# Scores of q's low parts as two 64-row matmuls, one on each half of the TensorE array

## The chip, the cores and the metric

One NeuronCore of a Trainium2 chip runs the whole program. The metric is the device time of one execution in microseconds. TensorE (PE in the profile) does matmuls and loads their weights (PEld), VectorE (DVE), ScalarE (ACT) and GpSimd (POOL) the rest; SyncE (SP) issues the DMAs.

## What is computed

Three blocks over 1024 tokens of width 1024. Two attentions over all keys are what the change is about:

```python
# layer 0, differential attention: 8 heads, two parts c of 64 per head
sc = jnp.einsum('bqhcd,bkhcd->bhcqk', qb, k, preferred_element_type=f32) * scale
p = jax.nn.softmax(sc, axis=-1)
p = p[:, :, 0] - lam * p[:, :, 1]
...
# layer 1, MLA: 8 heads, 128 features of their own and 64 roped ones, k_pe shared by the heads
sc = (jnp.einsum('bqhd,bkhd->bhqk', qn, k_nope, preferred_element_type=f32)
      + jnp.einsum('bqhr,bkr->bhqk', qp, k_pe, preferred_element_type=f32)) * scale
p = jax.nn.softmax(sc, axis=-1)
```

A third block follows (gating, causal and dilated attentions, an FFN), which the change leaves alone.

## The kernel before

Every fp32 operand x of a matmul is held as two fp32r tiles, a first part hi = round(x) and a second part lo = x - hi, so that a product is the sum of hi hi, hi lo and lo hi; `mm3` (L192) writes these three matmuls per 128 rows of contraction.

Where the contraction has 64 rows, the parts are stacked instead. In layer 0 `qk_rope` (L620) makes for each part s of a head the keys `kk[s]`, 128 rows by 1024 keys, with hi in rows 0 to 63 and lo in rows 64 to 127, and the queries `q[s](hl, j)`, 128 rows by 128 queries, in which the same part hl stands in both halves of the rows. It moves them there from the roped tiles `ab` by small DMAs on SP's queue (`move`, L675). `score` (L678) then needs two matmuls per 512 keys: q hi (L681) and q lo (L682) against the stack, all four products. A score row of `da_attention` (L847 on; 128 queries by 1024 keys, one PSUM tile `s` of two banks) is four matmuls; each of 8 heads has 8 query tiles times 2 parts, 128 rows in all. In layer 1 `mla_attention` (L1076) does the same for the 64 rope features with `kpe`, the stacked k_pe of all heads, and `qp`: per 512 keys three matmuls for the 128 features of the head (L1093 to L1095), then q's rope hi (L1096) and lo (L1097) against `kpe`. There a score row is ten matmuls, and there are 64.

A row then goes through `exp_row`: maximum on VectorE (L737, L738), exponential on ScalarE (L741), reciprocal (L742). `pt_fill` transposes it on TensorE (L757), ScalarE and VectorE split the transposes, and `pv` multiplies by v (L192). There are two PSUM tiles `s`.

Head h's attention is emitted in steps, with the projections of head h + 1 and the modulation of later layers as fill between them (`merge`, `alternate`); `ahead` lets the attention's instructions be scheduled before work emitted a little earlier. A list scheduler of the framework then sets the order on each engine from these priorities, so an edit of one matmul shifts others too. Within an engine and on SP's queue everything runs in that order.

The matmuls of few rows in the program before are in set-up alone: `columns` (L234) transposes vectors of 86, 56, 62, 88 and 44 rows, and `modulation_first` has sixteen one-row matmuls twice (L359).

Of the kernel before, what the change touches and what calls it, by code (L numbers as in the profile page):

```python
# [36 lines left out]
    dict(h4=20, kk=5, qq=5, ab=2, pt=12, e=6, v=3, z=3, wr=2, wh=3, wl=3, tb=3, t2=4, tf=3),  # L37
    dict(h4=18, kk=4, qq=6, ab=3, pt=12, e=6, v=3, z=3, wr=4, wh=3, wl=2, tb=3, t2=2, tf=4),
# [6 lines left out]
def alternate(a, b):  # L45
    """steps of a and of b together"""
    for _ in a:
        next(b, None)
        yield
    yield from b  # L50
# [7 lines left out]
def ahead(tc, gen, offset):  # L58
    """steps of gen, scheduled before work that was emitted up to offset instructions earlier"""
    if not offset:  # L60
        yield from gen
        return
    while True:
        with tc.high_priority(offset):
            x = next(gen, drain)
        if x is drain:
            return
        yield x


def some(g, n):
    """n steps of g"""
    for _ in range(n):
        if next(g, drain) is drain:
            return
        yield


def merge(main, fill, lead=0):
    """emit one step of fill after each step of main"""  # L80
    for _ in range(lead):
        next(fill, None)
    for _ in main:
        next(fill, None)
    drain(fill)


def pace(main, total, early, fill, n):
    """steps of early at once, then n steps of fill spread over main, whose steps give their weight"""
    w = done = 0  # L90
    for x in main:
        w += x or 1
        if next(early, 0) == 0:
            while done < n * w / total:
                next(fill, None)
                done += 1
    drain(early)
    drain(fill)


class Net:
# [18 lines left out]
    def load(self, tag, shape, dt=F32):  # L120
        """a tile to be loaded, but not long before its phase"""
# [10 lines left out]
    def t(self, tag, shape, dt=F32):  # L132
        """a tile of 4 KB a partition, seen in the shape"""
# [14 lines left out]
    def c(self, shape, name, dt=F32):  # L148
        """a constant, or columns that stay"""
        r = dt == F32R  # L150
        n = 1 if r else shape[1]
        if name not in self.where:
            self.where[name] = self.used[r]
            self.used[r] += n
        o = self.where[name]
        return self.cr[:, o] if r else self.cf[:, o:o + n]

    def small(self, cols, tag):
        """columns for a short time: the next of a few in turn"""
# [11 lines left out]
    def wblock(self, src, k, m, lo_eng=None):  # L171
        """src: DRAM [k*128, m]; returns [(hi, lo)] per contraction chunk, each [128, m]"""
        return self.wload([src], k, m, lo_eng)

    def wload(self, srcs, k, m, lo_eng=None):
        """blocks of columns side by side"""
# [10 lines left out]
    def mm3(self, out, ws, rs, start=True, stop=True):  # L187
        """out += sum_k ws[k]^T rs[k]; ws, rs: (hi, lo)"""
# [26 lines left out]
    def columns(self, tile_name, width, names):  # L215
        """vectors as columns [128, j]"""
# [23 lines left out]
    def mask_tile(self, name, op, pattern, mult):  # L240
        """0 where the condition holds, else -BIG"""
# [39 lines left out]
    def sigmoid(self, sg, z, src):  # L281
        """sg <- sigmoid(z); src: where |z| is read from (z or its PSUM source)"""
# [15 lines left out]
    def modulation(self, cs, w, bcol, names, acc_tag="t2", w_tag="wr", shared=()):  # L298
        """columns [128, 8] of each 1024 outputs of cs @ w + b; chunks in shared: on ScalarE and GpSimd"""
# [27 lines left out]
    def sum_cols(self, acc, out):  # L327
        """out [128, 8] <- sums over the partitions of acc"""
# [7 lines left out]
    def modulation_first(self, cs, w, bcol, g, nme, acc_tag, w_tag):  # L336
        """as modulation, half of the products on TensorE"""
# [24 lines left out]
    def scale_col(self, g, scale, name):  # L362
        """g * (1 + scale)"""
# [14 lines left out]
    def stat_sum(self, acc):  # L378
        """sum over partitions, on every partition (PSUM)"""
# [10 lines left out]
    def rsqrt_mean(self, out, sums, dim):  # L390
        """(sums / dim + eps)^-1/2"""
# [5 lines left out]
    def stat_end(self, acc, dim):  # L397
        """acc -> (sum over partitions / dim + eps)^-1/2 on every partition, in place"""
        return self.rsqrt_mean(acc, self.stat_sum(acc), dim)

    def new_xt(self, tags):
        """x^T of a token half: 8 chunks [128, 512] in len(tags) tiles"""
# [37 lines left out]
    def operand(self, x, tag="h4", eng=None):  # L440
        """x [128, 512], split"""
# [5 lines left out]
    def rows(self, w, c0, m=128):  # L447
        """loads columns c0.. of w as the rows of a block, by halves of the contraction"""
# [8 lines left out]
    def weights(self, load, early):  # L457
        """operands of two blocks of rows by the number of the product, the first two products' first"""
# [20 lines left out]
    def strassen(self, load, ops, box, tag, early=False):  # L479
        """two blocks of rows times h, [128, 1024] each; early: the products of the first token half, alone,  # L480
        in steps"""
# [31 lines left out]
    def next_h(self, proj, xbox, acc, acol, shift):  # L513
        """ends the projection; h of the next part (fp32, in the place of x), and the operands of its first
        token half"""
# [16 lines left out]
    def turn_ops(self, ops, b11, b12, b21, b22):  # L532
        """operands of a chunk of each half of the contraction, but the first two products'; in place"""
# [11 lines left out]
    def start_pairs(self, pair, n, chunk, ops):  # L545
        """the first pairs of blocks: what needs the first token half, the other operands, the rest"""
# [13 lines left out]
    def load_x(self):  # L560
        """tokens of x"""
# [8 lines left out]
    def turn_x(self, toks):  # L570
        """x^T of the token halves, and their normalisation as rows on every partition"""
# [31 lines left out]
    def rope_half(self, psa, psb, half, outs):  # L603
        """outs: Ah, Al, Bh, Bl views"""
# [15 lines left out]
    def qk_rope(self, w, qcol, kcol, hts, perm=1):  # L620
        """q, k of two 64-wide heads, roped, split and stacked for the scores: kk[s], q[s](hl, q tile)"""
# [18 lines left out]
        for half in range(2):  # L640
# [11 lines left out]
            for s in range(2):  # L652
# [4 lines left out]
                for d in range(2):  # L657
                    for i in range(2):
                        r = slice(64 * d + 32 * i, 64 * d + 32 * i + 32)
                        ks, qs = slice(64 + 32 * s, 96 + 32 * s), slice(32 * s, 32 * s + 32)  # L660
                        if perm == 1:
                            self.move(kk[s][r, half * 512:half * 512 + 512], ab[i][ks, d])
                            self.move(qt[s][half][r], ab[i][qs])
                        elif half:
# [13 lines left out]
    def score(self, ps, q, j, kk, ks, stop=True):  # L678
        """ps = q tile j . keys ks, all four products of the parts"""
# [4 lines left out]
    def v_tiles(self, w, cols, k, rs, perm=1, pair=False):  # L684
        """v [key, 128] of the columns, split: [128, hl, 8, 128], or pair: [128, 8, 2, hl, 64]"""
# [31 lines left out]
    def silu_blocks(self, w, cols, hts, box):  # L717
        """silu(h @ w[:, c:c + 128])^T for c in cols, fp32 [128, 1024]"""
# [14 lines left out]
    def exp_row(self, ps, scale):  # L733
        """softmax numerator and reciprocal of its sum"""
# [13 lines left out]
    def pt_fill(self, pts, p, slot, ktiles):  # L748
        """transposes of p[:, k tiles] into column slot; pts = [hi 0-1, lo 0-1, hi 2-3, ..]"""
# [14 lines left out]
    def pv(self, v, pts):  # L764
        """O^T [128, 512]"""
# [5 lines left out]
    def out_proj(self, w, ots, gcol, xs_in, xs_out, half, tags, stats, accs, box):  # L771
        """x' = x + gate * (o @ w) for a token half, in T layout; stats: column factors (or None) of accs"""
# [18 lines left out]
    def keep_o(self, o):  # L791
        """o^T chunk, split"""
# [11 lines left out]
    def load_o(self, od, half, cs, ots, fac=None):  # L804
        """chunks cs of o^T of a token half from DRAM, split"""
# [17 lines left out]
    def last_head(self, att, w0, w1, early, loads, proj, hold=0):  # L823
        """the attention of the last head; fill in its first half (of weight w0): early and the loads of
        the first half's o^T, in its second: the output projection of the first half (but hold steps,
        which come with the loads of the second half's o^T)"""
# [20 lines left out]
    def da_attention(self, h, kk, q, box, od, ots=None):  # L847
# [6 lines left out]
        for half in range(2):  # L854
            pts = self.pt_new()
            for slot in range(4):
                es = []
                for s in range(2):
                    ps = self.pS()
                    for kh in range(2):  # L860
                        ks = slice(kh * 512, kh * 512 + 512)
                        self.score(ps[:, ks], q[s], half * 4 + slot, kk[s], ks)
# [37 lines left out]
    def layer0(self):  # L900
# [25 lines left out]
        def qk(h, box):  # L926
            box.append((yield from self.qk_rope(w, h * 128, 1024 + h * 128, hts)))
# [41 lines left out]
    def lora_norm(self, w, c0, n, dim, gcol, hts, tags, box):  # L969
        """rmsnorm of h @ w[:, c0:c0+128n], as (hi, lo) tiles [half][block]"""  # L970
# [28 lines left out]
    def mla_kpe(self, w, c0, hts, kd):  # L999
        """roped k_pe^T stacked [hi (x1, x2); lo (x1, x2)]"""  # L1000
# [18 lines left out]
    def mla_qpe(self, wq, qa, qpe):  # L1019
        """roped q_pe of all heads -> DRAM [head, hl, 64, 1024]"""  # L1020
# [24 lines left out]
    def split_psum(self, ps, dst):  # L1045
        """dst [128, 2, 512] <- exact parts of ps"""
# [29 lines left out]
    def mla_attention(self, h, qn, qp, kn, vbox, kpe, zd, od, ots=None):  # L1076
        nc = self.nc
        scale = 192.0 ** -0.5
        for half in range(2):
# [4 lines left out]
            for slot in range(4):  # L1084
# [4 lines left out]
                for kh in range(2):  # L1089
# [7 lines left out]
                    nc.tensor.matmul(o, qp[1][:, qs], kpe[:, ks], start=False, stop=True)  # L1097
# [9 lines left out]
    def layer1(self, hts):  # L1107
# [34 lines left out]
        nc.sync.dma_start(kpe.bitcast(F32), kd)  # L1142
        od = self.scratch([8, 128, S], "od1")
# [11 lines left out]
        for h in range(7):  # L1155
            cur, box, vbox = box, [], []
            fill = alternate(chain(self.mla_v(h, a["w_kv_b"], ckv, vbox), head(h + 1, box)), some(mods, 4))
            merge(ahead(self.tc, self.mla_attention(h, *cur, vbox, kpe, zd, od), HP_M), fill)
        drain(mods)
        m2 = self.mod  # L1160
        for nme in ("gate_m", "gate_f"):
# [16 lines left out]
            self.mla_attention(7, *cur, vbox, kpe, zd, od, ots), 4, 4, self.mla_v(7, a["w_kv_b"], ckv, vbox),  # L1178
# [22 lines left out]
    def gelu(self, ps, dst):  # L1201
        """tanh-form gelu of ps into dst (SBUF)"""
# [11 lines left out]
    def mixer_a(self, w, hts, od):  # L1214
        nc, a = self.nc, self.a
        # causal w_sp, transposed and split
# [12 lines left out]
        for b in range(2):  # L1229
# [6 lines left out]
            # v: [s, g, n, c], group norm  # L1236
# [41 lines left out]
    def mixer_b_qk(self, w, p, hts, box):  # L1278
        """q, k of the heads of pair p"""
# [26 lines left out]
    def fold(self, ps, y, e):  # L1306
        """y rows of head e <- sum of the two row halves of ps"""
# [55 lines left out]
    def mixer_c_attention(self, g, d, kk, q, vbox, lse, od):  # L1363
# [4 lines left out]
        for e in range(2):  # L1368
# [61 lines left out]
            # lse = max * scale + ln(sum), 1 / sum; to token order  # L1430
# [17 lines left out]
    def alphas_c(self, lse, fac):  # L1448
        """softmax of lse over the 3 groups, over the softmax sum; [6, 1024] in token order"""
# [80 lines left out]
    def ffn(self, hs, ops):  # L1530
        """the convolved gate and val in pairs of blocks, and their product, kept in DRAM; then the product
        with w_down"""
# [47 lines left out]
    def down(self, half, k1, k2, act, ys):  # L1580
        """x + gate * (act @ w_down) for a token half, in T layout; ys: the chunks before k1"""
# [39 lines left out]
    def finish(self, xt, half):  # L1621
        """rmsnorm of x in token layout, with g_final"""
# [68 lines left out]
```

## Time and profile before

| | us |
|---|---|
| median of 3 runs | 3095.03 |
| lowest and highest run | 3091.07, 3096.70 |
| profiled execution, span from its first to its last instruction | 3102.5 |
| TensorE busy, matmul / weight load | 2673.2 (86%) / 2154.1 (69%) |
| VectorE busy | 2110.7 (68%) |
| ScalarE / GpSimd busy | 1434.4 (46%) / 1292.2 (42%) |
| layer 0's attention | about 90 to 786 |
| layer 1's attention | about 1100 to 1612 |

No other time of the profiled execution is given than its span; it is longer than the highest of the three runs by 5.8 us. Busy times are unions of an engine's instructions; the ends of matmuls are modelled, so that two that follow each other overlap in the list, and the distance from start to start is what one takes in a stream. The granted clock is the share of full speed (2.4 GHz) that TensorE was given; the lower of its two levels is 1.2 GHz.

### The profile page before, as it was taken

What the parts mean: (1) busy time and instruction counts of PE and PEld (TensorE: products, weight loads), DVE (VectorE), ACT (ScalarE), POOL (GpSimd) and SP (SyncE); (2) the same over time, 40 slices, a digit from 0 to 9 for tenths busy, and PEclk for the clock granted to TensorE, in tenths of its full rate; (3) what the DMA queues carried; (4) which work ended last, traced back from release to release, by engine and by line L of the source; (5) the groups of instructions that cost most, each with busy time, mean ns of one, the idle gap of its engine ahead of it and who ended that gap; (6) DMA issues with size and microseconds to landing.
All of it is one profiled execution on the core that took longest, in us unless ns stands there. A gap on an engine that the chain in (4) does not pass through costs nothing. (4 is left out here: it accounts for less than half of the span.)

```text
span 3102.5 us, 34630 instructions
## 1 busy us (share of the span) xinstructions
PE 2673.2 (86%) x12023; PEld 2154.1 (69%) x12023; DVE 2110.7 (68%) x2888; ACT 1434.4 (46%) x2609; POOL 1292.2 (42%) x775
## 2 busy tenths in 40 slices
PE   7899999999989957778789689888887999998897
PEld 4677777777767746567667567777675777776776
DVE  7787778766653365555566756377876888889865
ACT  5455554556444423334345444366743444444332
POOL 2323333223353522112124333244545877787761
PEclk8999999999999978889899899999998999998998
DMA  7433333224441352321334235533361222224664
GB/s 268 132 93 96 105 94 90 72 67 118 122 122 53 117 178 78 100 83 53 103 106 131 68 81 82 107 82 100 97 195 46 77 82 75 82 89 149 210 213 153
DMA packets 316225, 338.90 MB, mean 109 GB/s; under 512 B 37060, under 2 KB 239892, under 8 KB 316052
## 3 DMA queue, kind: packets, MB, share of 16 engines
q1 hardware_dynamic: 316052, 336.69, 37.0%
q8 instruction: 96, 1.57, 0.2%
q14 instruction: 77, 0.63, 0.1%
HBM read 231.17 MB, written 60.89 MB: 94 GB/s over the span
## 5 line engine op out<-in xcount | busy, mean ns | idle before, releaser
L192 PE MATMUL m<-h,wh 128*128 128x512 f32 x4744 | 1399.6, 404 | 59.3 <-ACT wh L183 18.6
L192 PEld LDWEIGHTS m<-h,wh 128*128 128x128 f32 x4744 | 912.1, 195 | 269.3 <-ACT wh L183 21.0
L192 PE MATMUL m<-h,wl 128*128 128x512 f32 x1472 | 590.3, 403 | 10.1 <-POOL wl L169 10.0
L169 POOL TENSOR_TENSOR wl<-wr,wh 128x1024 fp32r<-128x1024 f32 (+1 forms) x146 | 329.4, 2263 | 577.6 <-PE m L192 184.4
L761 ACT CAST pt<-m 128x256 fp32r<-128x256 f32 (+1 forms) x632 | 221.2, 369 | 367.8 <-DVE pt L169 192.1
L192 PEld LDWEIGHTS m<-h,wl 128*128 128x128 f32 x1472 | 286.5, 195 | 75.3 <-POOL wl L169 12.5
L169 DVE TENSOR_TENSOR pt<-m,pt 128x256 fp32r<-128x256 f32 (+2 forms) x652 | 256.8, 416 | 103.2 <-ACT pt L761 81.7
L741 ACT ACTIVATE e<-s,cf 128x1024 f32<-128x1024 f32 x192 | 214.8, 1120 | 163.6 <-DVE cf L738 140.2
L737 DVE TENSOR_REDUCE cf<-s 128x1 f32<-128x1024 f32 x192 | 232.6, 1218 | 70.6 <-PE s L682 38.6
L757 PE MATMUL m<-cr,e 128*128 128x128 f32 x1240 | 197.1, 285 | 61.3 <-DVE t L1104 31.4
L757 PEld LDWEIGHTS m<-cr,e 128*128 128x128 f32 x1240 | 155.3, 147 | 89.4 <-issue 53.4
L192 PE MATMUL s<-h,wh 128*128 128x512 f32 x720 | 182.8, 399 | 35.9 <-DVE h L169 17.1
L865 POOL TENSOR_SCALAR e<-e,cf 128x1024 f32<-128x1024 f32 x64 | 82.0, 1281 | 303.8 <-DVE cf L742 286.6
L681 PE MATMUL s<-kk,qq 128*128 128x512 f32 (+3 forms) x376 | 154.0, 415 | 51.6 <-ACT e L741 22.4
L1527 DVE SCALAR_TENSOR_TENSOR e<-z,cf,e 128x1023 f32<-128x1023 f32 (+1 forms) x88 | 175.8, 2008 | 24.8 <-ACT e L1525 24.6
L183 ACT CAST wh<-wr 128x1024 fp32r<-128x1024 f32 (+2 forms) x134 | 122.2, 915 | 145.5 <-PE m L192 67.6
L192 PE MATMUL m<-pt,v 128*128 128x512 f32 x768 | 187.7, 394 | 0.8 <-DVE pt L169 0.6
L192 PEld LDWEIGHTS s<-h,wh 128*128 128x128 f32 x720 | 136.3, 191 | 71.8 <-DVE h L169 18.9
L192 PEld LDWEIGHTS m<-pt,v 128*128 128x128 f32 x768 | 143.9, 189 | 31.6 <-DVE pt L169 1.5
L1099 POOL TENSOR_SCALAR e<-e,cf 128x1024 f32<-128x1024 f32 x64 | 72.8, 1141 | 213.8 <-DVE cf L742 210.0
L682 PE MATMUL s<-kk,qq 128*128 128x512 f32 (+3 forms) x376 | 146.0, 396 | 0.2 <-DMA qq<-pt 0.2
L169 DVE TENSOR_TENSOR wh<-wl,wh 128x512 fp32r<-128x512 f32 x90 | 120.6, 1358 | 19.1 <-ACT wh L443 19.0
(368 smaller groups left out, 4582.3 us busy)
## 6 DMA issues: line engine op xcount, KB each, us to landing
wr<-in_w_out_dram SPq DMA_DIRECT2D x48, 512.0 KB
tb<-in_w_ada_dram SPq DMA_DIRECT2D x48, 512.0 KB
wr<-in_w_up_dram SPq DMA_DIRECT2D x47, 512.0 KB
wr<-in_w_in_dram SPq DMA_DIRECT2D x45, 512.0 KB
qq<-ab SPq DMA_DIRECT2D x144, 128.0 KB
wr<-in_ada_w_dram SPq DMA_DIRECT2D x32, 512.0 KB
tf<-act SPq DMA_DIRECT2D x30, 512.0 KB
wr<-in_w_down_dram SPq DMA_DIRECT2D x30, 512.0 KB
```

What stands on the lines that cost most here:

```text
L169: (eng or self.nc.vector).tensor_sub(lo, src, hi.bitcast(F32))
L183: nc.scalar.copy(hi, raw)
L192: self.nc.tensor.matmul(out, l, r, start=start and n == 0, stop=stop and n == last)
L681: nc.tensor.matmul(ps, q(0, j), kk[:, ks], start=True, stop=False)
L682: nc.tensor.matmul(ps, q(1, j), kk[:, ks], start=False, stop=stop)
L737: nc.vector.reduce_max(nm, ps, axis=AX, negate=True)
L741: nc.scalar.activation(e, ps, AF.Exp, bias=nm, scale=scale, accum_out=sm)
L757: nc.tensor.transpose(ps[:, i], p[:, kt * 128:(kt + 1) * 128], self.ident)
L761: nc.scalar.copy(hi, ps[:, i:i + m])
L865: nc.gpsimd.tensor_scalar(e1, e1, r1, self.neglam, ALU.mult, ALU.mult)
L1099: nc.gpsimd.tensor_scalar(e, e, r, 1.0, ALU.mult, ALU.mult)
L1527: nc.vector.scalar_tensor_tensor(t[:, sh:], u[:, 0:S - sh], col(i), t[:, sh:], ALU.mult, ALU.add)
```

## The change

The product lo lo is left out, so q's second part needs only the first part of the keys, 64 rows. The two halves of the keys of a row are then one 64-row matmul each: keys 0 to 511 on rows 0 to 63 of the array, where `kk` and `kpe` have the first part already, keys 512 to 1023 on rows 64 to 127, for which a new tile `kx` holds the first part of these keys in the lower half of its rows. Each writes its own bank of the tile `s`. The 64-row matmuls come after the 128-row matmuls of both halves.

```diff
 CAPS = (
-    dict(h4=20, kk=5, qq=5, ...),
-    dict(h4=18, kk=4, qq=6, ...),
+    dict(h4=20, kk=5, kx=2, qq=5, ...),
+    dict(h4=18, kk=4, kx=1, qq=6, ...),
...
-    def qk_rope(self, w, qcol, kcol, hts, perm=1):
+    def qk_rope(self, w, qcol, kcol, hts, perm=1, kx=None):
...
                             self.move(kk[s][r, half * 512:half * 512 + 512], ab[i][ks, d])
                             self.move(qt[s][half][r], ab[i][qs])
+                            if kx is not None and half and d:
+                                self.move(kx[r, s * 512:s * 512 + 512], ab[i][ks, 0])
...
+    def score_row(self, ps, q, j, kk, kx):
+        nc = self.nc
+        halves = [ps[:, kh * 512:kh * 512 + 512] for kh in range(2)]
+        for kh in range(2):
+            nc.tensor.matmul(halves[kh], q(0, j), kk[:, kh * 512:kh * 512 + 512], start=True, stop=False)
+        self.low(halves, q(1, j), kk, kx)
+
+    def low(self, halves, q, kk, kx):
+        nc = self.nc
+        nc.tensor.matmul(halves[0], q[0:64], kk[0:64, 0:512], start=False, stop=True)
+        nc.tensor.matmul(halves[1], q[64:128], kx[64:128], start=False, stop=True)
...
     def da_attention(...):
...
-                    for kh in range(2):
-                        ks = slice(kh * 512, kh * 512 + 512)
-                        self.score(ps[:, ks], q[s], half * 4 + slot, kk[s], ks)
+                    self.score_row(ps, q[s], half * 4 + slot, kk[s], kx[:, s * 512:s * 512 + 512])
...
     def mla_attention(...):
...
                     nc.tensor.matmul(o, qp[0][:, qs], kpe[:, ks], start=False, stop=False)
-                    nc.tensor.matmul(o, qp[1][:, qs], kpe[:, ks], start=False, stop=True)
+                self.low([ps[:, 0:512], ps[:, 512:]], qp[1][:, qs], kpe, kx)
...
     def layer1(self, hts):
...
+        kx = self.t("kx", [128, 512], F32R)
+        nc.sync.dma_start(kx[64:128].bitcast(F32), kd[0:64, 512:])
```

In the changed kernel L740 is the matmul of q hi in `score_row`, L745 and L746 are the two of `low`, L679 is `move`, L773 the transposes of `pt_fill`; in the program's own tables L745 stands on rows 0 to 63 and L746 on rows 64 to 127, and the 56-, 62- and 44-row transposes of L234 on rows 0 to 63 likewise, in the same array mode of 64 rows.

On TensorE, in the attention of one of the middle heads of layer 0, two score rows before:

```order
L681 MATMUL s_2535<-kk_1841,qq_1949 128x512
L682 MATMUL s_2535<-kk_1841,qq_1949 128x512
L681 MATMUL s_2535<-kk_1841,qq_1949 128x512
L682 MATMUL s_2535<-kk_1841,qq_1949 128x512
L681 MATMUL s_2545<-kk_1842,qq_1958 128x512
L682 MATMUL s_2545<-kk_1842,qq_1958 128x512
L681 MATMUL s_2545<-kk_1842,qq_1958 128x512
L682 MATMUL s_2545<-kk_1842,qq_1958 128x512
L757 MATMUL m_2396<-cr,e_2381 128x128 x4
```

and two in the changed kernel:

```order
L740 MATMUL s_3247<-kk_2611,qq_2732 128x512 x2
L745 MATMUL s_3247<-kk_2611,qq_2732 128x512
L746 MATMUL s_3247<-kx_2596,qq_2732 128x512
L740 MATMUL s_3257<-kk_2612,qq_2741 128x512 x2
L745 MATMUL s_3257<-kk_2612,qq_2741 128x512
L746 MATMUL s_3257<-kx_2596,qq_2741 128x512
L386 MATMUL m_3146<-tf_3143,cr 128x512
```

The two halves of a row stand side by side, between 128-row work; this is so in 176 of the 192 rows of both layers (118 of 128 in layer 0, 58 of 64 in layer 1).

On TensorE at the beginning of a head of layer 0, in the changed kernel (`pt`, `v` belong to the head before):

```order
L740 MATMUL s_3162<-kk_2611,qq_2732 128x512
L745 MATMUL s_3162<-kk_2611,qq_2732 128x512
L740 MATMUL s_3172<-kk_2612,qq_2741 128x512
L745 MATMUL s_3172<-kk_2612,qq_2741 128x512
L773 MATMUL m_3071<-cr,e_3047 128x128
...
L192 MATMUL m_3115<-pt_2792,v_2441 128x512
L746 MATMUL s_3162<-kx_2596,qq_2732 128x512
L192 MATMUL m_3115<-pt_2791,v_2442 128x512
...
L746 MATMUL s_3172<-kx_2596,qq_2741 128x512
```

The second halves of the head's first rows come some 30 matmuls after the first halves, with 128-row work between and around them; 16 rows in all are split.

On SP's queue, the moves for a head of layer 0 in the changed kernel:

```order
L679 DMA kk_1858<-ab_2165 32x512
L679 DMA kk_1858<-ab_2166 32x512
L679 DMA kx_1843<-ab_2165 32x512
L679 DMA kx_1843<-ab_2166 32x512
L679 DMA kk_1859<-ab_2165 32x512
L679 DMA kk_1859<-ab_2166 32x512
L679 DMA kk_1859<-ab_2165 32x512
L679 DMA kk_1859<-ab_2166 32x512
L679 DMA kx_1843<-ab_2165 32x512
L679 DMA kx_1843<-ab_2166 32x512
L679 DMA qq_2178<-ab_2165 32x1024
L679 DMA qq_2178<-ab_2166 32x1024
```

Four moves of `kx` per head stand among the last moves of the keys, ahead of the last ones of q. Before there were none, the rest is as it was.

## Rows read from the trace of the kernel before

**Rows 1.** The page: span, busy time of each engine.
```profile
span 3102.5 us, 34630 instructions
PE 2673.2 (86%) x12023; PEld 2154.1 (69%) x12023; DVE 2110.7 (68%) x2888; ACT 1434.4 (46%) x2609; POOL 1292.2 (42%) x775
```

**Rows 2.** Busy time by stretch, layer 0's attention and layer 1's: start and end, length, then each engine's busy us and instructions, granted clock, DMA share, GB/s.
```profile
90.00:786.00 696.00, 633.01 (x2903) 508.06 (x2902) 507.60 (x883) 372.08 (x712) 214.51 (x117) 0.95 0.36 97
1100.00:1612.00 512.00, 385.66 (x1862) 315.32 (x1862) 276.06 (x552) 192.77 (x449) 96.29 (x87) 0.86 0.29 94
```

**Rows 3.** What TensorE waited for from 90 to 786 us: tile and line that waited, releaser, us in total, times, longest.
```profile
PE s L681 <- ACT e L741: 22.4, 14, 3.8
PE m L757 <- DVE cf L738: 14.6, 6, 4.6
PE m L757 <- DVE e L866: 6.4, 5, 1.8
PE s L681 <- DMA kk<-ab: 4.1, 2, 3.1
```

**Rows 4.** The same from 1100 to 1612 us.
```profile
PE s L1097 <- DMA h<-qpe: 36.6, 4, 10.0
PE m L757 <- DVE t L1104: 31.4, 2, 15.8
PE s L1094 <- DVE h L169: 23.4, 2, 17.5
PE m L192 <- DVE pt L169: 20.6, 3, 20.0
```

**Rows 5.** TensorE's matmuls in order of time, two score rows of layer 0: start us, us shown, line, operation, operands, rows*columns of the weights, shape.
```profile
508.19 0.39 PE L681 MATMUL s<-kk,qq 128*128 128x512 f32 x1
508.41 0.39 PE L682 MATMUL s<-kk,qq 128*128 128x512 f32 x1
...
509.77 0.39 PE L682 MATMUL s<-kk,qq 128*128 128x512 f32 x1
```

**Rows 6.** The weight loads of the same stretch; the load for the matmul that starts at 508.41 is the one at 508.19.
```profile
508.19 0.19 PEld L682 LDWEIGHTS s<-kk,qq 128*128 128x128 f32 x1
508.42 0.19 PEld L681 LDWEIGHTS s<-kk,qq 128*128 128x128 f32 x1
508.64 0.19 PEld L682 LDWEIGHTS s<-kk,qq 128*128 128x128 f32 x1
```

**Rows 7.** Matmuls in order of time around the transposes of 56 and 62 rows, which stand between two projections.
```profile
83.87 0.39 PE L192 MATMUL m<-h,wl 128*128 128x512 f32 x1
84.19 0.27 PE L234 MATMUL m<-cr,t 56*128 56x56 f32 x1
84.30 0.23 PE L234 MATMUL m<-cr,t 62*128 62x62 f32 x1
84.46 0.50 PE L192 MATMUL m<-h,wh 128*128 128x512 f32 x1
```

**Rows 8.** The weight loads of the same place (in brackets the loader's idle time before, and what released it).
```profile
83.65 0.19 PEld L192 LDWEIGHTS m<-h,wl 128*128 128x128 f32 x1
84.19 0.14 PEld L234 LDWEIGHTS m<-cr,t 56*128 56x128 f32 x1 [0.35 <-issue]
84.45 0.19 PEld L192 LDWEIGHTS m<-h,wh 128*128 128x128 f32 x1
84.56 0.19 PEld L192 LDWEIGHTS m<-h,wh 128*128 128x128 f32 x1
```

**Rows 9.** Matmuls and weight loads at two more returns to 128 rows: after one-row matmuls at 35.5 us, after a 44-row transpose at 2200.8 us.
```profile
33.03 2.57 PE L359 MATMUL m<-cf,t 1*128 1x1 f32 x16 [1.09 <-ACT t L356]
35.53 0.09 PEld L352 LDWEIGHTS s<-h,cf 128*1 128x1 f32 x2
...
2200.63 0.23 PE L234 MATMUL m<-cr,t 44*128 44x44 f32 x1 [0.27 <-DMA t<-in_conv_w_dram]
2200.78 0.42 PEld L757 LDWEIGHTS m<-cr,e 128*128 128x128 f32 x4
```

**Rows 10.** A 128-row transpose behind a score matmul: the matmul, the transpose, and the transpose's weight load.
```profile
518.21 0.39 PE L682 MATMUL s<-kk,qq 128*128 128x512 f32 x1
518.44 0.27 PE L757 MATMUL m<-cr,e 128*128 128x128 f32 x1
518.21 0.14 PEld L757 LDWEIGHTS m<-cr,e 128*128 128x128 f32 x1
```

**Rows 11.** Score matmuls of layer 1 in order of time, behind a wait of 8.81 us, at the lower clock level.
```profile
1322.94 0.63 PE L1094 MATMUL s<-h,h 128*128 128x512 f32 x1
1323.36 0.63 PE L1095 MATMUL s<-h,h 128*128 128x512 f32 x1
```

**Rows 12.** DMA queues of the page (packets, MB, share of 16 engines), and the moves of kk issued from 90 to 800 us (count, KB each).
```profile
q1 hardware_dynamic: 316052, 336.69, 37.0%
kk<-ab SPq DMA_DIRECT2D x124, 64.0 KB
```

More of the change, by code (lines that the diff above doesn't have):

```diff
@@ L36 @@
 CAPS = (
-    dict(h4=20, kk=5, qq=5, ab=2, pt=12, e=6, v=3, z=3, wr=2, wh=3, wl=3, tb=3, t2=4, tf=3),
-    dict(h4=18, kk=4, qq=6, ab=3, pt=12, e=6, v=3, z=3, wr=4, wh=3, wl=2, tb=3, t2=2, tf=4),
+    dict(h4=20, kk=5, kx=2, qq=5, ab=2, pt=12, e=6, v=3, z=3, wr=2, wh=3, wl=3, tb=3, t2=4, tf=3),
+    dict(h4=18, kk=4, kx=1, qq=6, ab=3, pt=12, e=6, v=3, z=3, wr=4, wh=3, wl=2, tb=3, t2=2, tf=4),
     dict(h4=18, kk=5, qq=4, ab=3, pt=8, e=5, v=4, z=3, wr=4, wh=3, wl=3, tb=2, t2=4, tf=4),
@@ L844, in last_head, with da_attention @@
         drain(loads[1])
-    def da_attention(self, h, kk, q, box, od, ots=None):
+    def da_attention(self, h, kk, q, kx, box, od, ots=None):
         nc = self.nc
@@ L926, in qk @@
         def qk(h, box):
-            box.append((yield from self.qk_rope(w, h * 128, 1024 + h * 128, hts)))
+            kx = self.t("kx", [128, S], F32R)
+            box.append((*(yield from self.qk_rope(w, h * 128, 1024 + h * 128, hts, kx=kx)), kx))
         def v(h, box):
@@ L1074, in mla_v, with mla_attention @@
         box.append((yield from self.v_tiles(wkv, h * 256 + 128, 2, ckv)))
-    def mla_attention(self, h, qn, qp, kn, vbox, kpe, zd, od, ots=None):
+    def mla_attention(self, h, qn, qp, kn, vbox, kpe, kx, zd, od, ots=None):
         nc = self.nc
@@ L1157, in layer1 @@
             fill = alternate(chain(self.mla_v(h, a["w_kv_b"], ckv, vbox), head(h + 1, box)), some(mods, 4))
-            merge(ahead(self.tc, self.mla_attention(h, *cur, vbox, kpe, zd, od), HP_M), fill)
+            merge(ahead(self.tc, self.mla_attention(h, *cur, vbox, kpe, kx, zd, od), HP_M), fill)
         drain(mods)
@@ L1177, in layer1 @@
         self.last_head(
-            self.mla_attention(7, *cur, vbox, kpe, zd, od, ots), 4, 4, self.mla_v(7, a["w_kv_b"], ckv, vbox),
+            self.mla_attention(7, *cur, vbox, kpe, kx, zd, od, ots), 4, 4, self.mla_v(7, a["w_kv_b"], ckv, vbox),
             [self.load_o(od, half, ((0, 1), (2, 3), (4, 5), (6,)), ots[half]) for half in range(2)], proj[0], 3)
```

## The prediction

> **What bounds the kernel now.** I read the page's engine totals first, then the two stretches that the change touches, then what TensorE waits for there, then single matmuls in order of time. TensorE is the busiest engine: 2673 of 3102.5 us, against 2111 for VectorE [rows 1]. In the attention of layer 0 (90 to 786 us) it works 633.0 of 696 us, or 91%, and no other engine is above 73%; in that of layer 1 (1100 to 1612 us) it works 385.7 of 512 us, or 75% [rows 2]. What it waits for in layer 0 is small and hangs on its own earlier work: 22.4 us until ScalarE's exponential has freed a score tile, 14.6 and 6.4 us for VectorE's results of score rows [rows 3]. In layer 1 the waits are few and long, up to 20.0 us: on q's rope parts coming back from DRAM, on VectorE [rows 4]. So time added on TensorE reaches the end almost in full in layer 0 and in good part in layer 1. As its share I take the share of the stretch that TensorE works: 0.91 and 0.75.
>
> **What a matmul costs there.** Eight score matmuls in a row start at 508.19 to 509.77 us: a slot of 1.58 / 7 = 0.226 us [rows 5]. Each is shown as 0.39 us long, since its tail lies under the next. What the next matmul needs is hidden too: its weight load starts with the matmul ahead of it, at 508.19, 508.42, 508.64 [rows 6]. A layer 0 row therefore costs 4 slots, a layer 1 row 10.
>
> **What the change removes and adds.** Per score row two 128-row matmuls, 2 x 0.226 = 0.452 us, become two 64-row ones on different halves of the array and into different banks. There are 128 rows in layer 0 (8 heads, 8 query tiles, 2 parts) and 64 in layer 1. If the two overlap fully and nothing else changes, a row gains one slot, 0.226 us. That is the bound on the gain.
>
> **What the array does when the number of rows changes** is the disputed price, and the trace of before has it at one place in the middle of a dense stream: two transposes of 56 and 62 rows (the set-up of small vectors), which stand on the same 64-row half as the new matmuls of the first key half. The last 128-row matmul ahead of them starts at 83.87 and is shown to end at 84.26. The weight load for the 56 rows does not start with it: it starts at 84.19, 0.07 us before that end, and the profile names no semaphore ("issue") for the 0.35 us in which the loader stood idle [rows 7, 8]. The way back is the same: the 62-row matmul starts at 84.30 and ends at 84.53, and the next 128-row load starts at 84.45, 0.08 before; only 0.11 later, at 84.56, is the load after that let in, which in the stream marks the moment when the first one's matmul begins to run [rows 7, 8]. Two further returns agree. After a 44-row transpose shown from 2200.63 to 2200.86 the 128-row load starts at 2200.78; after sixteen one-row matmuls that end at 33.03 + 2.57 = 35.60 the 128-row load starts at 35.53 [rows 9]. It isn't the kind of instruction: a transpose of 128 rows behind a score matmul has its load at 518.21, with the matmul ahead, and its own start one slot on, at 518.44 [rows 10]. So the weight load of another row count waits for the array to run empty, and then lies bare.
>
> The Trainium skill says the same without a price (TensorEngine Tiling (Array Packing), Key Properties: changing the tiling mode, not just the tile, drains the engine). What it adds to the row is that the drain belongs to 64-row mode as such and not to these few transposes.
>
> Worked out as an estimate from these rows, counted from the start of the last 128-row matmul: load of the first half at 0.39 - 0.07 = 0.32; its matmul runs from 0.43. I let the second half's load queue behind the first by the 0.11 us that one load takes, so its matmul runs from 0.54, overlapping the first. The next 128-row load waits for it: 0.54 + 0.32 = 0.86, its matmul runs from 0.97. Before, that matmul came 3 slots after, at 0.68. **A pair costs 0.97 - 0.68 = +0.29 us** instead of gaining. Bounds: with both halves running at once, 0.43 + 0.32 + 0.11 = 0.86, so +0.18; with no overlap at all, 0.43 + 0.226 + 0.43 = 1.09, so +0.41. I take +0.29, since all rows of before show loads one after another.
>
> The Trainium skill gives the friendlier bound (TensorE: Matmul & The Clock Gate, Measured speedup vs the span model): packed matmuls start about 4 ns apart. By it a pair would cost +0.18 us, and the total below would be 38 us instead of 55.
>
> **How many.** The change's order has 176 pairs back to back and 16 rows whose halves are split by 128-row work. In layer 0 these are 118 and 10, in layer 1 58 and 6; the split ones of layer 0 stand at the beginnings of heads, where the second half waits for the new copy of the keys. A lone 64-row matmul costs a switch in and out by itself: next 128-row work at 0.43 + 0.32 + 0.11 = 0.86 instead of 0.45, +0.41, twice per split row, +0.82.
>
> - Layer 0: 118 x 0.29 + 10 x 0.82 = 42.4 us on TensorE, x 0.91 = 38.6.
> - Layer 1: 58 x 0.29 + 6 x 0.82 = 21.7 us, x 0.75 = 16.3.
>
> Sum +55 us. With +0.18 a pair: 29.4 x 0.91 + 15.4 x 0.75 = 38. With +0.41: 56.6 x 0.91 + 28.7 x 0.75 = 73. Score matmuls that run at the lower clock level, with slots of 0.42 [rows 11], lose more; they are few and I add nothing.
>
> **The other edits.** 32 moves of 64 KB fill the copy kx in layer 0, one load fills it in layer 1: about 2 MB on 336.69 [rows 12], in stretches where the DMA engines are 0.36 and 0.29 busy [rows 2]: nothing by themselves. But they stand on SP's queue between the moves of kk and qq, and the moves behind them, q's among them, start later. The nearest price is the wait for kk: 4.1 us in 2 waits, the longest 3.1 [rows 3]. Bounds 0 to 7 later heads x 3.1 = 22 us; I take 0, since before only 2 waits on kk show in the whole stretch. If that cover goes, the first rows of a head are late, and ScalarE's exponential and the transposes behind them next. VectorE, ScalarE and GpSimd get the same operations as before.
>
> **Result.** The profiled execution spans 3102.5 us, 7.5 above the median of the runs, 3095.0. On the median, 3095 + 55 = 3150 us.
>
> **The rivals.**
> - *The pair pays* (other side). The drain at 84.19 would belong to those set-up transposes and not to a 64-row matmul in a stream. Then each pair gains up to a slot: 118 x 0.226 x 0.91 + 58 x 0.226 x 0.75 = 34 us, 3061; with the second load 0.11 late half of it, 3078. It is decided by the two switches of a pair: once they cost under 0.12 us together, a pair with staggered loads gains, and under 0.23 one that runs at once. For it: the halves share no rows and no bank. Against it: one entry and three returns, of three row counts, all with loads 0.07 to 0.08 us before the shown end [rows 7 to 9], which is 0.41 a round trip.
> - *No overlap.* The second half runs after the first: +73, 3168. No row shows two matmuls running at once, so nothing excludes it.
> - *The copy is late.* Besides the switches, heads wait for kx or the q moves: up to +22 on the forecast, 3172. For it: the split rows. Against it: 2 short waits on kk.
> - *Nothing to see.* The switches fall into waits, within 0.2% (6 us, about what a measurement of this kernel can tell from no change). In layer 0 the waits sum to under 10% of the stretch, and layer 1's are in a few places.
>
> **Chances.** Pairs at +0.18 to +0.41 with overlap: 0.62 (3133 to 3168). No overlap: 0.13. Late copy: 0.08. Little or nothing: 0.05 (0.04 within 0.2%, 0.01 just above). The pair pays: 0.12. Faster 0.12, same 0.04, slower 0.84. The forecast with its bounds takes 0.62 of 3133 to 3168; taking in no overlap, half of the late copy, and a share that reaches the end smaller than I took it (half of 38 to 55 us, 3114 to 3122), 3112 to 3182 holds about 8 in 10.
>
> **What would show it.** In the profile after, the weight loads of the first 64-row matmuls (line 745) start 0.07 us before the shown end of the matmul ahead, not with it; those of line 746 some 0.11 behind; the next 128-row load again 0.07 before the end of line 746's matmul. From the last 128-row matmul ahead of a pair to the first behind it I expect about 0.97 us. Layer 0's attention takes some 39 us longer, layer 1's some 16, the rest nothing. TensorE waiting for kx would be the late copy. Wrong it is if the load of line 745 starts with the matmul ahead, or if line 746 starts a slot after line 745.

## The result

The changed kernel takes 3135.7 us (median of 4 runs, 3126.8 to 3143.6) against 3093.2 us of before (median of 4): a ratio of 1.0138, 95% interval 1.0115 to 1.0160, or +43 us. It is slower, as forecast; the forecast was 3150 (3112 to 3182).

The profile after. Its page has the same work on every engine but TensorE, whose matmuls are busy 38 us longer and whose weight loads 47 us shorter than in [rows 1] (the loads of the two halves lie over each other and count once):

```profile
span 3130.1 us, 34717 instructions
PE 2711.1 (87%) x12023; PEld 2107.6 (67%) x12023; DVE 2109.3 (67%) x2888; ACT 1437.5 (46%) x2609; POOL 1296.7 (41%) x775
```

The two profiled executions lie only 27.6 us apart (3102.5 and 3130.1), less than the medians: behind layer 1's attention, where the change edits nothing, the one after is 8 us shorter. So the profile tells where time went, and the runs tell how much.

By stretch, layer 0's attention, which now ends at 819 us, and layer 1's, from 1135 to 1648; the columns are those of [rows 2]:

```profile
90.00:819.00 729.00, 664.56 (x2905) 483.11 (x2903) 508.26 (x884) 371.96 (x712) 212.82 (x117) 0.93 0.35 96
1135.00:1648.00 513.00, 402.43 (x1862) 301.17 (x1862) 279.07 (x555) 194.16 (x449) 96.88 (x86) 0.86 0.29 95
```

Layer 0 grew from 696 to 729 us, TensorE's busy time in it by 31.5: nearly all of it is TensorE's. In layer 1 TensorE is busy 17 us more, and the stretch grew by 1. The matmuls of one pair, in order of time, and then the weight loads of the same place:

```profile
430.40 0.39 PE L740 MATMUL s<-kk,qq 128*128 128x512 f32 x1
430.72 0.50 PE L745 MATMUL s<-kk,qq 64*128 64x512 f32 x1
430.72 0.50 PE L746 MATMUL s<-kx,qq 64*128 64x512 f32 x1
431.15 0.50 PE L740 MATMUL s<-kk,qq 128*128 128x512 f32 x1
```

```profile
430.72 0.18 PEld L745 LDWEIGHTS s<-kk,qq 64*128 64x128 f32 x1 [0.35 <-issue]
430.72 0.18 PEld L746 LDWEIGHTS s<-kx,qq 64*128 64x128 f32 x1
431.15 0.19 PEld L740 LDWEIGHTS s<-kk,qq 128*128 128x128 f32 x1 [0.24 <-ACT ab L617]
431.26 0.19 PEld L740 LDWEIGHTS s<-kk,qq 128*128 128x128 f32 x1
```

The last 128-row matmul starts at 430.40 and is shown to 430.79. The 64-row loads start at 430.72, 0.07 before that end, after 0.35 us of the loader's idle time that no semaphore explains: the entry of [rows 7, 8] again. Both halves load and run at once. The matmuls are shown to 431.22; the next 128-row load starts at 431.15, and the load after it at 431.26, when its matmul begins to run. From 430.40 to 431.26 are 0.86 us, against 3 slots of 0.226 before: +0.18 a pair, the lower bound of the forecast.

The profile puts the 0.24 us ahead of the load at 431.15 down to an operation of ScalarE. But of the 207 returns from 64 to 128 rows in this trace, 141 show such an idle time (0.245 us in the median) with no semaphore, so it belongs to the return. The place is typical otherwise too. I counted from the last 128-row matmul's start to the second one behind, where all have 512 columns: the 82 such pairs at 2.4 GHz cost +0.18 us in the median, 14 lone 64-row matmuls +0.40, and 14 pairs at 1.2 GHz, in slots of 0.43, +0.17.

What TensorE waited for in layer 1, against [rows 4]:

```profile
PE m L773 <- DVE t L1119: 33.4, 2, 16.7
PE s L745 <- DMA h<-qpe: 28.6, 5, 7.1
PE s L1109 <- DVE h L169: 23.7, 2, 17.8
PE s L1108 <- ACT e L757: 22.9, 4, 12.3
```

The wait for q's rope parts shrank from 36.6 to 28.6 us, and the 20.6 us for VectorE's parts at L192 are gone from the top; the wait on the exponential grew from 4.2 us to 22.9. So the profile alone leaves open whether layer 1's switches are free or paid for by something else. In layer 0 nothing waits for kx; the waits for kk, 4.1 us in [rows 3], are these:

```profile
PE s L740 <- DMA kk<-ab: 4.8, 3, 3.4
```

### The profile page after: what moved, and what is told of

The parts are those of the page before. It is cut to its first block, busy times and chain, and to the rows that moved or that the text cites. A ratio compares the mean times of both kernels' runs of the same rounds, so it can differ in the third digit from the quotient of the medians.

```text
span 3130.1 us, 34717 instructions
## 1 busy us (share of the span) xinstructions
PE 2711.1 (87%) x12023; PEld 2107.6 (67%) x12023; DVE 2109.3 (67%) x2888; ACT 1437.5 (46%) x2609; POOL 1296.7 (41%) x775
## 5 line engine op out<-in xcount | busy, mean ns | idle before, releaser
L192 PE MATMUL m<-h,wh 128*128 128x512 f32 x4744 | 1399.0, 404 | 63.5 <-ACT wh L183 15.9
L192 PEld LDWEIGHTS m<-h,wh 128*128 128x128 f32 x4744 | 910.9, 195 | 273.7 <-ACT wh L183 17.6
L192 PE MATMUL m<-h,wl 128*128 128x512 f32 x1472 | 590.9, 403 | 10.4 <-POOL wl L169 10.4
L192 PEld LDWEIGHTS m<-h,wl 128*128 128x128 f32 x1472 | 286.7, 195 | 75.2 <-POOL wl L169 12.5
L773 PE MATMUL m<-cr,e 128*128 128x128 f32 x1240 | 202.3, 289 | 56.2 <-DVE t L1119 33.4
L192 PE MATMUL s<-h,wh 128*128 128x512 f32 x720 | 183.1, 400 | 36.2 <-DVE h L169 17.9
L773 PEld LDWEIGHTS m<-cr,e 128*128 128x128 f32 x1240 | 154.3, 148 | 85.3 <-issue 62.1
L192 PE MATMUL m<-pt,v 128*128 128x512 f32 x768 | 198.3, 408 | 1.2 <-DVE pt L169 0.6
L192 PEld LDWEIGHTS s<-h,wh 128*128 128x128 f32 x720 | 137.0, 192 | 72.3 <-DVE h L169 19.6
L192 PEld LDWEIGHTS m<-pt,v 128*128 128x128 f32 x768 | 146.9, 196 | 39.6 <-issue 6.1
L1361 POOL TENSOR_TENSOR e<-e,tb 128x128 f32<-128x128 f32 (+7 forms) x48 | 78.6, 1643 | 121.5 <-ACT tb L1360 90.7
L443 ACT CAST wh<-wl 128x512 fp32r<-128x512 f32 x120 | 72.3, 617 | 99.9 <-DVE e L1544 24.9
```

The lines of the kernel that those rows point to most:

```text
L192: self.nc.tensor.matmul(out, l, r, start=start and n == 0, stop=stop and n == last)
L443: self.nc.scalar.copy(t[:, 0], x)
L773: nc.tensor.transpose(ps[:, i], p[:, kt * 128:(kt + 1) * 128], self.ident)
L1361: nc.gpsimd.tensor_mul(u, u, stay)
```

## The experiments

The theory: the array runs empty at each change of the number of rows, and that is the price. Its rivals: the new order of the matmuls, the moves of kx, or halves that don't overlap. The granted clock is one more, which no run holds still. All ratios are to the kernel before, run beside each; 0.1% is 3.1 us.

**No switches, all else kept (wide).**
```diff
-        nc.tensor.matmul(halves[0], q[0:64], kk[0:64, 0:512], start=False, stop=True)
-        nc.tensor.matmul(halves[1], q[64:128], kx[64:128], start=False, stop=True)
+        nc.tensor.matmul(halves[0], q, kk[:, 0:512], start=False, stop=True)
+        nc.tensor.matmul(halves[1], q, kk[:, 512:1024], start=False, stop=True)
```
Expected: 

> The change with its two 64-row matmuls made 128-row again (q's low part against both parts of the keys, as before the change), in the place and order of the change, and with the 33 DMAs that fill kx kept. Theory, the switch of the array's mode is the whole price: no 64-row matmul, so within 6 us of before (3093). Rival, the new order and the moves of kx are a good part of the price: 3105 to 3135.

Measured: 3086.4 us, ratio 0.9985 (0.9973 to 0.9996). Without 64-row matmuls the change costs nothing, it even gains 5 us. So the 64-row mode as a whole costs 47 us (1.0138 against 0.9985), and the new order and the moves together cost nothing. Layer 0's attention and what follows it, with nearly the same number of matmuls, in the kernel before, the change and wide (columns as in [rows 2]):

```profile
90.00:899.00 809.00, 736.44 (x3339) 590.46 (x3338) 575.33 (x962) 422.76 (x794) 266.91 (x144) 0.95 0.37 103
90.00:931.00 841.00, 767.31 (x3341) 565.44 (x3339) 576.04 (x963) 422.60 (x794) 265.35 (x144) 0.93 0.37 102
90.00:909.00 819.00, 739.44 (x3346) 594.07 (x3344) 577.04 (x962) 423.61 (x794) 262.31 (x144) 0.94 0.38 104
```

TensorE's busy time is back to within 3 us of before. The granted clock lies between the two others.

**Halves that can't overlap (same_half).**
```diff
-        nc.tensor.matmul(halves[1], q[64:128], kx[64:128], start=False, stop=True)
+        nc.tensor.matmul(halves[1], q[0:64], kk[0:64, 512:1024], start=False, stop=True)
```
Expected: 

> The change with both 64-row matmuls on rows 0 to 63 of the array, so that they can't run side by side; the moves of kx stay. Theory, the two halves of the change do run at once (their starts lie 3 ns apart in its profile): each pair costs one slot more, 0.86 + 0.23 = 1.09 us from the last 128-row matmul to the first behind the pair, 178 pairs x 0.226 = 40 us on TensorE, 30 to 40 of them at the end: 3165 to 3175. Rival, the starts are modelled and the halves run one after the other already: same as the change, 3136.

Measured: 3164.5 us, 1.0234 (1.0221 to 1.0247), 30 us above the change by the ratios, the lower end of what was expected. So the two halves of the change do overlap. Matmuls and weight loads of one pair:

```profile
422.51 0.40 PE L740 MATMUL s<-kk,qq 128*128 128x512 f32 x1
422.83 0.50 PE L745 MATMUL s<-kk,qq 64*128 64x512 f32 x1
423.17 0.39 PE L746 MATMUL s<-kk,qq 64*128 64x512 f32 x1
```

```profile
422.83 0.18 PEld L745 LDWEIGHTS s<-kk,qq 64*128 64x128 f32 x1 [0.37 <-issue]
422.94 0.19 PEld L746 LDWEIGHTS s<-kk,qq 64*128 64x128 f32 x1
423.49 0.53 PEld L773 LDWEIGHTS m<-cr,e 128*128 128x128 f32 x5 [0.36 <-issue]
```

On the same rows the second load comes 0.11 us behind the first, its matmul a slot (0.23) behind the first one's run, and the next 128-row load at 423.49, 0.98 after 422.51 where the change has 0.75. With the 0.11 us of that load it is 1.09, the forecast's bound without overlap. On different rows the second load need not queue: that is what the forecast had wrong.

**One layer at a time (layer0_only, layer1_only).** In each the other layer keeps `score` or L1097 as before, and no kx.

Expected of layer 0 alone: 

> The change in layer 0 alone, layer 1 as before. Theory from the traces, in which layer 0's attention grew by 32 us and layer 1's by 2: 3121 to 3129. Rival, both layers pay in proportion to their rows (2 to 1): 3122 here, but 3107 in the kernel with layer 1 alone.

Expected of layer 1 alone: 

> The change in layer 1 alone, layer 0 as before. Theory, the waits of layer 1 (q's rope parts from DRAM, VectorE) take in what the switches add: 3093 to 3099. Rival, in proportion to its rows: 3107 (0.75 of 64 x 0.18 plus the split rows would be 3104.5).

Measured: layer 0 alone 3131.3 us, 1.0135 (1.0119 to 1.0151); layer 1 alone 3088.0 us, 0.9989 (0.9979 to 0.9999). The first is 2 us above its expected range, the second 5 below, outside of both theories. The whole loss shows in layer 0. I had put the missing loss of layer 1 down to its waits; the next kernels say otherwise.

**The order alone, by layer (l1_wide, l0_wide, l0_order).** These undo the 64-row mode as in wide, in the kernels with one layer changed; l0_order also drops the moves of kx:
```diff
-            kx = self.t("kx", [128, S], F32R)
-            box.append((*(yield from self.qk_rope(w, h * 128, 1024 + h * 128, hts, kx=kx)), kx))
+            box.append((*(yield from self.qk_rope(w, h * 128, 1024 + h * 128, hts)), None))
```
Expected of layer 1's order: 

> Layer 0 as before; in layer 1 the order of the change (q's low rope part against both key halves after the other eight matmuls) with 128-row matmuls as before. Theory, layer 1 looked free in the change because its order gives back what the switches take: the wait for q's rope parts from DRAM falls due later, and the attention of layer 1 shrinks by about 15 to 20 us: 3072 to 3080. Rival, the switches of layer 1 fell into waits that are there anyway and the order is worth nothing: 3088 to 3095.

Expected of layer 0's order and moves: 

> Layer 1 as before; in layer 0 the order of the change (first parts of both key halves, then low parts) and the 32 moves of kx, with 128-row matmuls as before. Theory, order and moves cost layer 0 some 10 us by themselves, the switches the other 30 of the 40 measured: 3100 to 3106. Rival, the 40 us are switches alone: 3089 to 3095.

Expected of layer 0's order without the moves: 

> Layer 1 as before; layer 0 with the order of the change and 128-row matmuls, without the 32 moves of kx. Theory, the moves on SP's queue ahead of q's are what layer 0 pays besides the switches (14 us with order and moves): within 4 us of before, 3089 to 3097. Rival, the order itself, first parts of both key halves ahead of any low part, costs it: 3100 to 3110 again.

Measured: layer 1's order 3064.5 us, 0.9910 (0.9897 to 0.9924), 28 us faster, more than expected; layer 0's order and moves 3109.6 us, 1.0044 (1.0031 to 1.0057), 4 us above what was expected; without the moves 3114.2 us, 1.0074 (1.0061 to 1.0087), nearer to the rival. So:

- Layer 1: the order gives 28 us, and with the switches 3 are left: the switches cost 24. They were not hidden in waits. What the order gives is waiting alone: before, TensorE was busy as long (499.5 us) in a stretch of 648 us, 1100 to 1748, as it is here in 618. What TensorE waited for with the order alone, 1103 to 1721 us, shows 15 us less for q's rope parts and 12 less at L192 than [rows 4]:

```profile
PE m L773 <- DVE t L1120: 31.6, 2, 15.9
PE s L1110 <- DVE h L169: 23.3, 2, 17.4
PE s L745 <- DMA h<-qpe: 21.8, 5, 6.8
...
PE m L192 <- DVE pt L169: 8.9, 5, 6.8
```

  The same stretch with the order alone and with the switches too (l1_wide, layer1_only):

```profile
1103.00:1721.00 618.00, 499.50 (x2342) 406.32 (x2342) 372.62 (x669) 258.74 (x554) 154.27 (x117) 0.89 0.33 104
1104.00:1741.00 637.00, 517.71 (x2342) 394.41 (x2342) 375.04 (x671) 259.49 (x555) 157.23 (x118) 0.88 0.32 101
```

  The switches keep TensorE busy 18 us longer there, and the stretch is 19 us longer.
- Layer 0: of 42 us the order costs 14 with the moves (the switches are the other 28), 23 without them. The moves are not the price; that expectation fell. The order's cost is for the most part waiting: without the moves, the stretch that took 809 us before (90 to 899) takes 830 (90 to 920), with TensorE busy 740.5 us against 736.4. Why fewer DMAs come out 9 us slower these runs don't show; it may be the schedule, which every edit shifts. I take some 10 us either way as what such a shift can be worth, an estimate from this one pair. The two orders together give -14 us by the sum and -5 in wide, within that uncertainty.

**Fewer switches, the same 64-row matmuls (two_rows).** Layer 0 alone, the pairs of both score rows of a query tile pinned behind the 128-row matmuls of both:
```diff
                 for s in range(2):
+                    self.low(rows[s][1], q[s](1, j), kk[s], kx[:, s * 512:s * 512 + 512], True)
+                for s in range(2):
+                    es.append(self.exp_row(rows[s][0], 0.125))
```
Expected: 

> Layer 1 as before; in layer 0 the 64-row pairs of the two score rows of a query tile are issued together behind the 128-row matmuls of both, so that the array changes its mode 76 times instead of 137, with the same 64-row matmuls. Theory, the price is per switch: from the last 128-row matmul to the first behind the four, 0.43 + 0.23 + 0.43 = 1.09 us, where five 128-row slots took 1.13, so the gain of the pairs just pays the switch; 9 us for the rows that stay split, and the order's 10: 3100 to 3112. Rival, each 64-row matmul costs by itself, or the clock is what costs: about 3131 as with layer 0 changed alone.

Measured: 3172.7 us, 1.0254 (1.0237 to 1.0271). Both theories missed it. Where four 64-row matmuls stand together the price per switch holds, matmuls and then loads:

```profile
318.67 0.39 PE L881 MATMUL s<-kk,qq 128*128 128x512 f32 x1
318.99 0.49 PE L746 MATMUL s<-kk,qq 64*128 64x512 f32 x1
...
319.32 0.39 PE L746 MATMUL s<-kk,qq 64*128 64x512 f32 x1
```

```profile
319.09 0.19 PEld L746 LDWEIGHTS s<-kk,qq 64*128 64x128 f32 x1
319.10 0.19 PEld L747 LDWEIGHTS s<-kx,qq 64*128 64x128 f32 x1
319.64 0.42 PEld L707 LDWEIGHTS m<-cr,tf 128*128 128x128 f32 x4 [0.36 <-issue]
```

The second pair's loads are pulled ahead (319.09), it runs a slot behind the first, and the next load starts 0.97 us after 318.67 (0.99 in the median of the 41 such groups at 2.4 GHz). With 0.11 us for that load, about 1.09 us go by where 128-row matmuls took five slots, 1.13: a gain of 0.04. But the two score tiles now fill together, and TensorE stands waiting for the softmax of their rows, from 90 to 860 us:

```profile
PE m L774 <- DVE e L889: 49.6, 24, 7.8
PE s L881 <- ACT e L758: 36.8, 18, 5.8
```

In [rows 3] these are 6.4 and 22.4, in the kernel with layer 0 changed alone 5.0 and 15.1: 66 us more waiting than there, where the time grew by 37 (by the ratios). So the trace shows the grouping to break even on the array, and these waits make it a loss in this pipeline of two score tiles. Its end time doesn't test the price of a switch; that it is paid per switch and not per matmul rests on the trace.

**What layer 1's order gave back (l1_rope_last, qp_early, l1_wide_qp_early).** The first puts both rope products behind the six others of both halves, in 128-row matmuls; the others move the two loads of `qp` in `mla_head` to its beginning:
```diff
+        qp = [...]                     # the two loads of q's rope parts
         ws = self.wblock(wq[:, h * 192:h * 192 + 128], 3, 128)
...
-        qp = [...]
```
Expected of both rope products last: 

> As the kernel with layer 1's order alone, and q's first rope part too after the six matmuls of the head's own features. Theory, the later the rope parts are needed the less of their DMA is waited for: at or below that kernel, 3065 to 3078. Rival, its wait is behind by then and only the order of the low part mattered: the same as that kernel.

Expected of the early loads: 

> The kernel before, with the two loads of q's rope parts of a head issued ahead of the weights of its projection, not behind. Theory, TensorE's wait for these loads (36.6 us in four waits before) is what layer 1's order gave back in part (15 us less wait): with the loads early 10 to 30 us faster, 3063 to 3083, without any change of order. Rival, the wait moves to the next late thing (VectorE's parts of keys and values): 3086 to 3096.

Expected of early loads and order: 

> Layer 1's order of the change with 128-row matmuls, and the early loads of q's rope parts. Theory, both act on the same wait, of which 21.8 us are left with the order alone: 3045 to 3062 against 3065. Rival, what is left is bound by VectorE: 3060 to 3068.

Measured: both rope products last 3078.3 us, 0.9948 (0.9936 to 0.9960); early loads 3043.5 us, 0.9841 (0.9827 to 0.9856); early loads and order 3031.2 us, 0.9798 (0.9784 to 0.9811). The last two are faster than either theory expected. That later is better is wrong: both products last are 12 us slower than the low one alone. Its wait for q's rope parts is as short (21.2 us), but the 20 us wait of L192 is back:

```profile
PE m L192 <- DVE pt L169: 22.1, 5, 19.6
PE s L745 <- DMA h<-qpe: 21.2, 4, 6.6
```

Early loads are worth 49 us, more than the 36.6 that TensorE was seen to wait for them, and none of that wait is left. Two more waits of [rows 4] go with it: that on L1104 is down from 31.4 us to 0.5 and that at L192 from 20.6 to 0.4. In their place others have grown; what TensorE waits for longest with early loads alone, 1103 to 1700 us, is:

```profile
PE s L1093 <- ACT e L741: 37.9, 6, 23.9
PE s L1093 <- DVE h L169: 28.0, 1, 28.0
```

The first was 4.2 us before. With the order on top the gain is 62 us, 2%: the best version here, with no 64-row matmul in the attentions.

## Why the prediction was right

- **The switch: right.** The drain and the bare load stand in the trace of after with the numbers read from four places of before, 0.32 in and 0.32 out and 0.11 for a load. The rival that it belongs to the set-up transposes is out.
- **The second half's load: wrong.** "I let the second half's load queue behind the first by the 0.11 us that one load takes": it loads at once, +0.18 and not +0.29 a pair. Only loads on the same rows queue, as same_half shows. The row of before that I leaned on had two transposes on the same rows. The Trainium skill's span model (TensorE: Matmul & The Clock Gate, Measured speedup vs the span model), by which packed matmuls start about 4 ns apart, was right here; by the rows both matmuls start at 430.72.
- **The sum: partly luck.** The forecast priced the switches alone, at 55 us, or 38 with +0.18. By wide against the change they cost 47. The new order has no term in my sum, yet its two parts, +14 in layer 0 and -28 in layer 1, were each as large as a layer's share. That the total of 43 lies near the forecast comes from errors that stand against each other: a load priced too high, against shares of 0.91 and 0.75 that were too low (33 us of stretch for 31.5 on TensorE in layer 0, 19 for 18 in layer 1), a clock that I left out and an order that happened to give back what it took.
- **Layer 0:** forecast 38.6 (26.8 with +0.18); alone it measured 42, of which the switches are 28. On TensorE the profile after shows 31.5 us more, against 29.4 with +0.18 and 42.4 in the forecast.
- **Layer 1:** forecast 16.3 (11.5); the switches cost 24 and the order gave 28. The share of 0.75 was too low: of 18 us more on TensorE all reached the end of the stretch, which grew by 19. The rest of the 24 lies behind the stretch, where neither kernel is edited; it is within the 10 us that two schedules may differ by, and its cause stays open.
- **The moves of kx: right**, nothing waits for them. The late copy did not happen, and the lone 64-row matmuls of the split rows cost the +0.40 us of their switches (0.41 in the forecast).
- **The clock: left out.** In layer 0's attention the granted clock fell from 0.95 to 0.93, with less of the time at 2.4 GHz and more at 1.2. In the trace 142 matmuls of this stretch start at the lower level before and 211 after. With slots of 0.42 us there [rows 11] against 0.23, these 69 lose at most some 13 us, an estimate; transposes are shorter and lose less. Whether the switches bring the clock down no run shows, so a part of their 28 us may come by way of it. My remark that score matmuls at the lower level lose more did not hold: a pair costs +0.17 us there and +0.18 at 2.4 GHz.

## What to carry to other kernels

Two matmuls on the two halves of the array take one slot, but the change of mode around them has a price: here, at 2.4 GHz, the way into 64-row mode and back cost about 0.41 us, nearly two slots of a 512-column fp32r matmul (0.45). So one pair between 128-row matmuls lost 0.18 us, and two pairs behind each other only broke even. Find one place in the old trace where the number of rows changes and read the weight loads there, not the matmuls: a load that doesn't start with the matmul ahead shows the drain. And when a change also reorders matmuls, run the order alone first: here its two parts were worth 14 and 28 us, against 43 for the change, and it led to a late DMA whose earlier issue gave 49.

## What the runs showed of the hardware that was not expected

- Weight loads for the two halves of the array start together (430.72 both), on one half 0.11 us apart (422.83, 422.94). Within the mode they are pulled ahead under the running matmul as with 128 rows: the second pair's loads start at 319.09 and 319.10, when the first pair begins to run, and its matmuls follow at 319.32.
- Two 64-row matmuls of 512 columns into two banks take one slot together: the change and the kernel with both on one half differ by 0.23 us a pair in the trace (0.75 and 0.98) and by 30 us in time.
